# A fp32 encoder block on one core: weight loads through eight half-size buffers, with the pair loads in quarters

## The chip, the core and the metric

The kernel runs on one core of a Trainium2 chip. TensorE (PE) multiplies, with its weight loads shown as PEld; VectorE (DVE) and ScalarE (ACT) work on tiles in SBUF, which has 128 partitions; GpSimd (POOL) does a little; SyncE (SP) issues nearly all of the DMAs, one after another. The metric is the device time of one execution in microseconds, the median of several runs. Below, "us" is microseconds.

## What is computed

One layer of an encoder on 256 tokens of width 2048, in float32. The reference, cut to the order of the stages:

```
hn = rmsnorm(h, mix_norm_pre)
z, xbc, dt_raw, u = split(hn @ w_in)
mix = concat([ssd_mixer(z, xbc, dt_raw, ...), pool_mixer(u, ...)]) @ w_out
h = h + rmsnorm(mix, mix_norm_post)
hn = rmsnorm(h, ffn_norm_pre)
gate, val = split(hn @ w_ffn_up)                  # 2048 x 11264
ff = (gelu(dwconv(gate)) * val) @ w_ffn_down      # 5632 x 2048
h = h + rmsnorm(ff, ffn_norm_post)
gate = sigmoid(rmsnorm(h, ple_norm_pre) @ w_ple_gate)
h = h + rmsnorm(gate * (p @ w_ple), ple_norm_post)
```

Some 252 MB of weights and inputs are read from HBM in one execution.

## The kernel before

**Products.** Every weight tile is split in two parts: `split` (L147) casts it on ACT to a rounded high part (L152, names ending in `whi`) and subtracts that from it on DVE for the low part (L153, `wlo`). Activations are kept as such pairs too. A product of two fp32 matrices is then three products on PE: high x high, high x low, low x high, accumulated in PSUM. `mm` (L87) issues them all.

**Stages.** `w_in` first (names `dtu`, `xb`, `z`), then the mixers, then `wo` (the output projection), the FFN (`ug` and `uv`, the two halves of the up-projection, into `ga` and `va`), `dn` (the down-projection) and `gt` (the gate of the last step). In `dn` the output has two halves of 1024 columns, `dn0` and `dn1`; each runs over 22 units, and a unit is two row blocks of 128 rows by 1024 columns, 1 MB of weights. The number behind `dn0` or `dn1` in a name is the unit's first row block: `dn116` is unit 8 of the second half. PE writes its plain results to `dna` and four helper results to `dns`.

**Seven products.** Units 1, 3, 5, 6, 8, 10, 11, 13, 15, 16 (and 18 in the second half) of `dn`, and three units of `wo`, treat their 256 x 1024 weights as a 2 x 2 matrix of blocks b11, b12, b21, b22 of 128 x 512 and multiply in seven products instead of eight (`seven_products`, L224). This takes two weight combinations f and g (`weight_sums`, L214: one DVE operation for f, two for g) and sums of the activations (`hs`). The sums are made in the FFN stage, stored to DRAM, loaded back (`sums`, 256 KB) and split again. For the units with u % 5 = 3 (3, 8, 13, 18) f and g are made in `dn` from the raw load. For the others they are made in the FFN stage (`block_ahead`, from loads named `br`), stored, and loaded back as `bm` (1 MB); of the weights themselves `three_blocks` (L162) then loads only b12 and the row b21, b22.

The order of the seven is s4, a12 (both with the tile split from b21 and b22), a11 (with b11 or what stands for it), s1, s3 (f, the tile `c`), s2, a22 (g, the tile `d`), three matmuls of 128 x 512 each, on PE in this order.

**Buffers and queues.** A load goes to one of four raw buffers of 128 x 2048 (tag `raw`, 8 KB in each partition, L157 to L168). A buffer is free when the last operation on it has ended, and the load that waits for it blocks SP, with all loads behind it: SP's queue is in order. The split parts have five buffers each (tags `whi`, `wlo`), free when PE has read them. DMAs count on eight semaphores in turn, so each waits for the landing of the eighth before it. The scheduler of the tile framework lays each engine's instructions in one fixed order when the kernel is built, and the engines follow it in order.

**Front.** The first stage loads `x` in transposed form to three buffers (`xt0`, a raw buffer `xt1`, a page `xt2`; a page is another kind of buffer, 128 x 2048, 14 of them) and `w_in`'s columns for `dtu` to raw buffers and pages in turn.

Of the kernel before, what the change touches and what calls it, by code (L numbers as in the profile page):

```python
# [16 lines left out]
P = 128  # L17
L = 256
# [33 lines left out]
def build(nc, a, out):  # L52
# [5 lines left out]
    with tile.TileContext(nc) as tc, \  # L58
# [35 lines left out]
        make_identity(nc, ident)  # L94

        c_dt = DSSD + 1536
        r0 = wp.tile([P, 2048], F32, tag="raw", bufs=4, name="dtur0")
# [9 lines left out]
        for i in range(16):  # L107
            nc.tensor.transpose(warm[:, :P], ident, ident)

        xt = [ep.tile([P, V_SCW + L], F32, name="xt0")] + [wp.tile([P, 2048], F32, tag="raw", bufs=4, name="xt1"), page("xt2")]  # L110
        vt = cp.tile([P, V_N - V_SCW], F32, name="vt")
        small = ep.tile([P, 89 + 512], F32, name="small")

# [2 lines left out]
        def load(dst, src, ahead=False):  # L116

            with tc.issue_after(last["dma"]) if last and not ahead else nullcontext():
                return ins(nc.sync.dma_start(dst, src))

        def x_part(k):
            return xt[0][:, V_SCW:] if k == 0 else xt[1 + k // 9][:, (k - 1) % 8 * L:((k - 1) % 8 + 1) * L]

        def xload(k0, k1):
            c = ((k0 - 1) % 8) * L
            last["dma"] = load(xt[1 + k0 // 9][:, c:c + (k1 - k0) * L],
                               a["x_cols"][:, V_SCW + k0 * L:V_SCW + k1 * L])

        last["dma"] = load(xt[0], a["x_cols"][:, :V_SCW + L])
        dtb, alog, dsk = small[:, :32], small[:, 32:64], small[:, 64:80]  # L130
# [23 lines left out]
                c0 = c1  # L154
            return hi, lo

        def raw(name, src, a_, b_):  # L157
            r = wp.tile([P, 2048], F32, tag="raw", bufs=4, name=name)
            last["dma"] = load(r[:, :a_ * b_].rearrange("p (a b) -> p a b", a=a_), src, True)
            return r  # L160

        def three_blocks(name, w, k0, c0):  # L162

            r = wp.tile([P, 2048], F32, tag="raw", bufs=4, name=name)
# [48 lines left out]

        def weight_sums(name, r, dst=None):  # L214

            v = r.rearrange("p (b c) -> p b c", b=4)
            f, g = dst or (mid(f"{name}f"), mid(f"{name}g"))
            nc.vector.tensor_sub(f.rearrange("p (b c) -> p b c", b=2), v[:, 1:3],
                                 v[:, 0].unsqueeze(1).to_broadcast([P, 2, 512]))
            nc.vector.tensor_add(g[:, :512], v[:, 2], f[:, :512])  # L220
            nc.vector.tensor_sub(g[:, 512:], v[:, 3], g[:, :512])
            return f, g

        def seven_products(name, r, a_, acc, alt, start, stop, made=None):  # L224

            b2 = split(parts(f"{name}b"), r[:, 1024:], 0, 1024)
            b11 = split(parts(f"{name}a"), r[:, 512:], 0, 512)
            with tc.issue_after(last["dve"]) if name.startswith("wo") else nullcontext():
                f, g = made or weight_sums(name, r)
            t13, t24 = (split(parts(f"{name}{n}"), x, 0, 1024) for n, x in (("c", f), ("d", g)))  # L230
            for x, (wh, wl), c, o, own in (
                    ("s4", b2, 0, acc[0][0], False), ("a12", b2, 1, acc[0][1], False), ("a11", b11, 0, alt[0], True),
                    ("s1", t13, 0, alt[1], True), ("s3", t13, 1, alt[2], True), ("s2", t24, 0, alt[3], True),
                    ("a22", t24, 1, acc[1][1], False)):
# [19 lines left out]
            add(acc[1][0], acc[1][0], s165)  # L254
            add(acc[1][1], acc[1][1], s167)

        def pair_of_rows(w, k0, c0):
            return w[k0 * P:(k0 + 2) * P, c0:c0 + 1024].rearrange("(k p) c -> p k c", p=P), 2, 1024

        def split_two(name, w, k0, c0):  # L260

            r = raw(f"{name}r{k0}", *pair_of_rows(w, k0, c0))
            return [(k0 + j, *split(parts(f"{name}{k0}_{j}"), r[:, j * 1024:(j + 1) * 1024], 0, 1024)) for j in range(2)]

        def token_major(name, w, c0, ks, get, acc, tail=1, fast=(), alt=None, sums=None, hooks={}, made=None):


            group, nu, sums_of = [], len(ks) // 2, {}
            for u in range(nu):
                k0 = ks[2 * u]  # L270
                if u + 1 in fast:
                    sums_of[u + 1] = sums(ks[2 * u + 2])
                if u in fast:
                    sets = made(u, c0)
                    r = three_blocks(f"{name}r{k0}", w, k0, c0) if sets else raw(f"{name}r{k0}", *pair_of_rows(w, k0, c0))
# [24 lines left out]
        def feature_major(name, w, c0, get, acc):  # L300

            for u in range(4):
                r = raw(f"{name}r{u}", w[u * 512:(u + 1) * 512, c0:c0 + 512]
                        .rearrange("(k p) c -> p k c", p=P), 4, 512)
                tiles = []

                def step(j, kk, f):
# [5 lines left out]
                           k == 0 and q == 0 and f % 2 == 0, k == NK - 1 and q == 2)  # L313

                for j in range(2):
                    tiles.append(split(parts(f"{name}{u}_{j}"), r[:, j * 1024:(j + 1) * 1024], 0, 1024))
# [11 lines left out]
        def feature_pairs(name, w, c0, get, acc):  # L328
# [14 lines left out]
                        for kk in range(4) for f in range(2)]  # L343

            for u in range(2):
                r = raw(f"{name}r{u}", w[u * 1024:(u + 1) * 1024, c0:c0 + 256]
                        .rearrange("(k p) c -> p k c", p=P), 8, 256)
                tiles = []
                for j in range(2):
                    behind = held.pop((name, u, j), None)  # L350
                    with tc.issue_after(behind) if behind else nullcontext():
                        tiles.append(split(parts(f"{name}{u}_{j}"), r[:, j * 1024:(j + 1) * 1024], 0, 1024))
# [106 lines left out]


        for u in range(0, NK, 2):
            r = [wp.tile([P, 2048], F32, tag="raw", bufs=4, name=f"dtur{u}") if u else r0, page(f"dtur{u + 1}")]
            for j in range(2):
                k = u + j
                if k == 0:
# [6 lines left out]
                if k == 1:  # L472
                    xload(2, 4)
                elif k in (3, 5, 7):
                    xload(*{3: (4, 9), 5: (9, 13), 7: (13, 16)}[k])
# [349 lines left out]

        def wo_block(u):

            r = raw(f"wb{u}", *pair_of_rows(w_out, wo_ks[2 * u], 1024))
            v = page(f"wf{u}")
            wo_sets[u] = weight_sums(f"wb{u}", r, (v[:, :1024], v[:, 1024:]))  # L830

# [98 lines left out]

        def block_ahead(u, half):

            r = raw(f"br{u}_{half}", *pair_of_rows(w_down, 2 * u, half * 1024))
# [4 lines left out]
        def block_made(u, c0):  # L938
# [200 lines left out]
```

## Time and profile before

| | us |
|---|---|
| median of 3 runs | 1118.2 (1117.71 to 1118.35) |
| the profiled execution | 1121.51 |
| its span, first to last instruction | 1119.7 |
| PE busy | 1105.8 |
| DVE busy | 830.5 |
| ACT busy | 679.6 |

The profile is of one execution, the granted TensorE clock in it is 0.998 of full speed. Its parts are: busy time by engine, the span in slices, DMA queues, the chain of work that ended last (followed back from the end, at each step to what released it), the costliest groups of instructions, and the DMA issues with the time from issue to landing. Timelines give single instructions; a bracket at the end of a row tells how long the engine was idle before it and what released it. Times in rows are counted from the span's start.

### The profile page before, as it was taken

What the parts mean: (1) busy time and instruction counts of PE and PEld (TensorE: products, weight loads), DVE (VectorE), ACT (ScalarE), POOL (GpSimd) and SP (SyncE); (2) the same over time, 40 slices, a digit from 0 to 9 for tenths busy, and PEclk for the clock granted to TensorE, in tenths of its full rate; (3) what the DMA queues carried; (4) which work ended last, traced back from release to release, by engine and by line L of the source; (5) the groups of instructions that cost most, each with busy time, mean ns of one, the idle gap of its engine ahead of it and who ended that gap; (6) DMA issues with size and microseconds to landing.
All of it is one profiled execution on the core that took longest, in us unless ns stands there. A gap on an engine that the chain in (4) does not pass through costs nothing.

```text
span 1119.7 us, 15690 instructions
## 1 busy us (share of the span) xinstructions
PE 1105.8 (99%) x6032; PEld 962.3 (86%) x6032; DVE 830.5 (74%) x1040; ACT 679.6 (61%) x999; POOL 51.9 (5%) x80
## 2 busy tenths in 40 slices
PE   9999999999999999999999999999999999999996
PEld 9999988888788888888888888888888887877885
DVE  6668887879776876767767767666887787897574
ACT  6757884555865564655565656555666465657462
POOL 0300022100200000000000000000000000001001
PEclk9999999999999999999999999999999999999999
DMA  9954446666587977877897797676788778886742
GB/s 354 376 171 151 152 151 241 211 211 225 215 281 246 310 257 253 275 266 254 264 305 252 244 318 258 213 247 214 262 292 289 268 270 304 296 283 218 241 136 76
DMA packets 145739, 275.69 MB, mean 246 GB/s; under 512 B 5504, under 2 KB 98560, under 8 KB 142208
## 3 DMA queue, kind: packets, MB, share of 16 engines
q1 hardware_dynamic: 145376, 274.33, 72.8%
q8 instruction: 47, 0.77, 0.3%
q10 hardware_dynamic: 288, 0.36, 0.1%
q14 instruction: 28, 0.23, 0.1%
HBM read 251.86 MB, written 22.81 MB: 245 GB/s over the span
## 4 chain that ended last, share of the span: by engine, by line
PE 85%; DMA 7%; DVE 3%; ACT 2%; issue 2%; POOL 0%; SPq 0%; DVEq 0%; POOLq 0%; ACTq 0%
PE va L87 22%; PE ga L87 21%; PE dna L87 10%; PE gt L87 7%; PE woa L87 7%; PE xbc L87 6%; PE z L87 4%; PE dns L87 3%; DMA sums<-sums 2%; DMA dtur<-w_in 2%; DMA xb2r<-w_in 1%; DMA x<-x 1%; DMA dn1r<-w_ffn_down 1%; PE wos L87 1%; DVE dn_1wlo L153 1%
## 5 line engine op out<-in xcount | busy, mean ns | idle before, releaser
L87 PE MATMUL ga<-wox,ug_0whi 128*128 128x512 f32 x352 | 87.8, 391 | 0.0
L87 PE MATMUL va<-wox,uv_0whi 128*128 128x512 f32 x352 | 87.6, 391 | 0.0
L87 PE MATMUL ga<-wox,ug_1whi 128*128 128x512 f32 x352 | 87.2, 389 | 0.0
L87 PE MATMUL va<-wox,uv_1whi 128*128 128x512 f32 x352 | 86.9, 389 | 0.0
L87 PEld LDWEIGHTS va<-wox,uv_1whi 128*128 128x128 f32 x352 | 66.1, 188 | 13.7
L87 PEld LDWEIGHTS ga<-wox,ug_1whi 128*128 128x128 f32 x352 | 66.0, 188 | 13.7
L87 PEld LDWEIGHTS va<-wox,uv_0whi 128*128 128x128 f32 x352 | 64.6, 188 | 12.4
L87 PEld LDWEIGHTS ga<-wox,ug_0whi 128*128 128x128 f32 x352 | 64.6, 188 | 12.3
L87 PE MATMUL ga<-wox,ug_1wlo 128*128 128x256 f32 x352 | 49.7, 283 | 0.9 <-DVE ug_1wlo L153 0.9
L87 PE MATMUL ga<-wox,ug_0wlo 128*128 128x256 f32 x352 | 49.5, 283 | 0.0
L87 PE MATMUL va<-wox,uv_1wlo 128*128 128x256 f32 x352 | 49.4, 283 | 0.0
L87 PE MATMUL va<-wox,uv_0wlo 128*128 128x256 f32 x352 | 49.2, 283 | 0.0
L87 PEld LDWEIGHTS ga<-wox,ug_0wlo 128*128 128x128 f32 x352 | 46.8, 191 | 1.8
L87 PEld LDWEIGHTS va<-wox,uv_0wlo 128*128 128x128 f32 x352 | 46.7, 191 | 1.7
L87 PEld LDWEIGHTS ga<-wox,ug_1wlo 128*128 128x128 f32 x352 | 45.4, 192 | 1.3 <-DVE ug_1wlo L153 1.3
L87 PEld LDWEIGHTS va<-wox,uv_1wlo 128*128 128x128 f32 x352 | 45.4, 192 | 0.0
L87 PE MATMUL xbc<-hnh,xb_0whi 128*128 128x256 f32 x96 | 27.6, 288 | 0.3 <-ACT u L539 0.3
L864 POOL TENSOR_SCALAR dnm<-dnq,fmean 128x1 f32<-128x1 f32 x2 | 0.6, 282 | 587.5 <-ACT dnj L861 587.5
L87 PE MATMUL xbc<-hnh,xb_1whi 128*128 128x256 f32 x96 | 27.5, 287 | 0.0
L87 PE MATMUL xbc<-hnh,xb_0wlo 128*128 128x256 f32 x96 | 27.3, 284 | 0.0
L87 PE MATMUL xbc<-hnh,xb_1wlo 128*128 128x256 f32 x96 | 27.2, 283 | 0.0
L87 PE MATMUL xbc<-hnl,xb_1whi 128*128 128x256 f32 x96 | 27.2, 283 | 0.0
(1654 smaller groups left out, 3084.4 us busy)
## 6 DMA issues: line engine op xcount, KB each, us to landing
dn0r<-w_ffn_down SPq DMA_DIRECT2D x15, 1024.0 KB, 7.3
dn1r<-w_ffn_down SPq DMA_DIRECT2D x15, 1024.0 KB, 7.2
br<-w_ffn_down SPq DMA_DIRECT2D x14, 1024.0 KB, 5.5
bm<-block SPq DMA_DIRECT2D x14, 1024.0 KB, 5.5
zr<-w_in SPq DMA_DIRECT2D x8, 1024.0 KB, 5.2
wo0r<-w_out SPq DMA_DIRECT2D x8, 1024.0 KB, 6.0
gt0r<-w_ple_gate SPq DMA_DIRECT2D x8, 1024.0 KB, 5.9
gt1r<-w_ple_gate SPq DMA_DIRECT2D x8, 1024.0 KB, 5.5
```

The costliest lines, as they stand in the source:

```text
L87: last["pe"] = ins(nc.tensor.matmul(o, lhsT, rhs, start=start, stop=stop, skip_group_check=True))
L153: last["dve"] = ins(nc.vector.tensor_sub(lo[:, s], src[:, s], hi[:, s].bitcast(F32)))
L864: nc.gpsimd.tensor_scalar(m, q, 1.0 / D, mean[t], op0=ALU.mult, op1=ALU.add)
```

## The change

The four raw buffers of 128 x 2048 become eight of 128 x 1024, and each load of 1 MB becomes two or more, each into a buffer of its own with its own release.

- `split_two` (pairs of row blocks), `feature_major`, `feature_pairs` and the loads of `bm` take two loads of 512 KB in place of one of 1 MB.
- `four_blocks` takes the place of `three_blocks`, and of the whole load where f and g are made from it (`dn`, `block_ahead`, `wo_block`): four loads of 128 x 512 (256 KB), three where b11 isn't used. One buffer, r[1], holds b12 and b21; the other, r[0], holds b11 and b22. b12 and b21 are loaded first, then b22, then b11.
- `seven_products` splits r[1] whole first (tile `b`), then the b22 half of r[0] (tile `a`). s4 takes the second half of `b`, a12 the tile `a`, a11 the first half of `b`. f takes r[1] less b11, in one operation as before.
- In the front `xt1` and `xt2` become four half buffers, `dtur` lies in pages throughout, and one load of `x` is cut in two.

```
-            r = wp.tile([P, 2048], F32, tag="raw", bufs=4, name=name)
+            return wp.tile([P, 1024], F32, tag="raw", bufs=8, name=name)
...
-            load(r[:, 512:1024], w[k0 * P:(k0 + 1) * P, c0 + 512:c0 + 1024], True)
-            last["dma"] = load(r[:, 1024:], w[(k0 + 1) * P:(k0 + 2) * P, c0:c0 + 1024], True)
+            r = [buffer(f"{name}{i}") for i in range(2)]
+            for i, c, k in ((1, 0, 0), (1, 1, 1), (0, 1, 1), (0, 0, 0)):
+                if all_ or (i, c) != (0, 0):
+                    w0 = c0 + (c if i == 0 else 1 - c) * 512
+                    last["dma"] = load(r[i][:, c * 512:(c + 1) * 512], w[(k0 + k) * P:(k0 + k + 1) * P, w0:w0 + 512], True)
...
-            nc.vector.tensor_sub(f.rearrange("p (b c) -> p b c", b=2), v[:, 1:3],
-                                 v[:, 0].unsqueeze(1).to_broadcast([P, 2, 512]))
+            nc.vector.tensor_sub(f.rearrange("p (b c) -> p b c", b=2), r[1].rearrange("p (b c) -> p b c", b=2),
+                                 r[0][:, :512].unsqueeze(1).to_broadcast([P, 2, 512]))
...
-            b2 = split(parts(f"{name}b"), r[:, 1024:], 0, 1024)
-            b11 = split(parts(f"{name}a"), r[:, 512:], 0, 512)
+            mid_ = split(parts(f"{name}b"), r[1], 0, 1024)
+            end_ = split(parts(f"{name}a"), r[0], 512, 1024)
...
-                    ("s4", b2, 0, acc[0][0], False), ("a12", b2, 1, acc[0][1], False), ("a11", b11, 0, alt[0], True),
+                    ("s4", mid_, 1, acc[0][0], False), ("a12", end_, 1, acc[0][1], False), ("a11", mid_, 0, alt[0], True),
...
-            r = raw(f"{name}r{k0}", *pair_of_rows(w, k0, c0))
-            return [(k0 + j, *split(parts(f"{name}{k0}_{j}"), r[:, j * 1024:(j + 1) * 1024], 0, 1024)) for j in range(2)]
+            two = []
+            for k in (k0, k0 + 1):
+                r = raw(f"{name}r{k}", w[k * P:(k + 1) * P, c0:c0 + 1024])
+                two.append((k, *split(parts(f"{name}{k0}_{k - k0}"), r, 0, 1024)))
+            return two
...
-                r = raw(f"bm{x[0]}_{x[1]}", block[x].unsqueeze(1), 1, 2048)
-                return r[:, :1024], r[:, 1024:]
+                return [raw(f"bm{x[0]}_{x[1]}{i}", block[x][:, i * 1024:(i + 1) * 1024]) for i in range(2)]
```

SP's queue grows from 338 to 541 rows. The order on the other engines moves only in places. On DVE, in the second half of `dn` before the change, the splits of unit 6 (`dn112`: tiles b, a, c, d) stand ahead of f for unit 8 (`dn116f`), and the splits of unit 7 (`dn114_0`, `dn114_1`) behind it:

```order
L153 TENSOR_TENSOR dn112bwlo_8674<-dn1r12_8665,dn112bwhi_8673 128x1024
L153 TENSOR_TENSOR dn112awlo_8678<-dn1r12_8665,dn112awhi_8677 128x512
L153 TENSOR_TENSOR dn112cwlo_8682<-bm6_1_8671,dn112cwhi_8681 128x1024
L153 TENSOR_TENSOR dn112dwlo_8686<-bm6_1_8671,dn112dwhi_8685 128x1024
L218 TENSOR_TENSOR dn116f_8759<-dn1r16_8746 128x1024
L153 TENSOR_TENSOR dn114_0wlo_8715<-dn1r14_8712,dn114_0whi_8714 128x1024
L153 TENSOR_TENSOR dn114_1wlo_8719<-dn1r14_8712,dn114_1whi_8718 128x1024
```

The same place on DVE after the change:

```order
L162 TENSOR_TENSOR dn112bwlo_9079<-dn1r121_9067,dn112bwhi_9078 128x1024
L162 TENSOR_TENSOR dn112awlo_9083<-dn1r120_9066,dn112awhi_9082 128x512
L162 TENSOR_TENSOR dn112cwlo_9087<-bm6_10_9074,dn112cwhi_9086 128x1024
L230 TENSOR_TENSOR dn116f_9170<-dn1r161_9154,dn1r160_9153 128x1024
L162 TENSOR_TENSOR dn112dwlo_9091<-bm6_11_9076,dn112dwhi_9090 128x1024
L162 TENSOR_TENSOR dn114_0wlo_9120<-dn1r14_9117,dn114_0whi_9119 128x1024
L162 TENSOR_TENSOR dn114_1wlo_9126<-dn1r15_9123,dn114_1whi_9125 128x1024
```

f of unit 8 now stands one row earlier, ahead of the last split of unit 6. The same happens at f of units 3, 8 and 13 in the first half and 13 and 18 in the second. On ACT, in the second half of `dn` before the change, between the casts of g of unit 13 (`dn126d`) and of unit 15 (`dn130b`), `hs30` is the cast of unit 15's sums and `dn128` is unit 14:

```order
L152 CAST dn126dwhi_8983<-dn126g_8975 128x1024
L152 CAST dn128_0whi_9012<-dn1r28_9010 128x1024
L152 CAST hs30_9049<-sums30_9008 128x512
L152 CAST dn128_1whi_9016<-dn1r28_9010 128x1024
L152 CAST dn130bwhi_9054<-dn1r30_9046 128x1024
L152 CAST dn130awhi_9058<-dn1r30_9046 128x512
L152 CAST hs32_9094<-sums32_9044 128x512
```

The same place on ACT after the change:

```order
L161 CAST dn126dwhi_9410<-dn126g_9402 128x1024
L161 CAST hs30_9480<-sums30_9435 128x512
L161 CAST dn128_0whi_9439<-dn1r28_9437 128x1024
L161 CAST hs32_9529<-sums32_9473 128x512
L161 CAST dn128_1whi_9445<-dn1r29_9443 128x1024
L161 CAST dn130bwhi_9487<-dn1r301_9476 128x1024
L161 CAST dn130awhi_9491<-dn1r300_9475 128x512
```

The cast of `hs30` moves ahead of the first cast of unit 14, and that of `hs32` (unit 16) ahead of the second one; in the first half both move the same way. In the FFN the order on ACT and DVE stays, and PE's order stays but for the tiles `a` and `b` in the seven products.

More of the change, by code (lines that the diff above doesn't have):

```diff
@@ L96, in build, with buffer @@
         c_dt = DSSD + 1536
-        r0 = wp.tile([P, 2048], F32, tag="raw", bufs=4, name="dtur0")
+        def buffer(name):
+            return wp.tile([P, 1024], F32, tag="raw", bufs=8, name=name)
+        r0 = page("dtur0")
         for n in range(2):
@@ L108, in build @@
             nc.tensor.transpose(warm[:, :P], ident, ident)
-        xt = [ep.tile([P, V_SCW + L], F32, name="xt0")] + [wp.tile([P, 2048], F32, tag="raw", bufs=4, name="xt1"), page("xt2")]
+        xt = [ep.tile([P, V_SCW + L], F32, name="xt0")] + [buffer(f"xt{i}") for i in range(1, 5)]
         vt = cp.tile([P, V_N - V_SCW], F32, name="vt")
@@ L119, in load, with x_place @@
                 return ins(nc.sync.dma_start(dst, src))
+        def x_place(k):
+            return 1 + (k - 1) // 4, (k - 1) % 4 * L
         def x_part(k):
-            return xt[0][:, V_SCW:] if k == 0 else xt[1 + k // 9][:, (k - 1) % 8 * L:((k - 1) % 8 + 1) * L]
+            if k == 0:
+                return xt[0][:, V_SCW:]
+            i, c = x_place(k)
+            return xt[i][:, c:c + L]
         def xload(k0, k1):
-            c = ((k0 - 1) % 8) * L
-            last["dma"] = load(xt[1 + k0 // 9][:, c:c + (k1 - k0) * L],
-                               a["x_cols"][:, V_SCW + k0 * L:V_SCW + k1 * L])
+            i, c = x_place(k0)
+            last["dma"] = load(xt[i][:, c:c + (k1 - k0) * L], a["x_cols"][:, V_SCW + k0 * L:V_SCW + k1 * L])
         last["dma"] = load(xt[0], a["x_cols"][:, :V_SCW + L])
@@ L155, in split, with raw, four_blocks @@
             return hi, lo
-        def raw(name, src, a_, b_):
-            r = wp.tile([P, 2048], F32, tag="raw", bufs=4, name=name)
-            last["dma"] = load(r[:, :a_ * b_].rearrange("p (a b) -> p a b", a=a_), src, True)
-            return r
-        def three_blocks(name, w, k0, c0):
-            r = wp.tile([P, 2048], F32, tag="raw", bufs=4, name=name)
-            load(r[:, 512:1024], w[k0 * P:(k0 + 1) * P, c0 + 512:c0 + 1024], True)
-            last["dma"] = load(r[:, 1024:], w[(k0 + 1) * P:(k0 + 2) * P, c0:c0 + 1024], True)
+        def raw(name, src, a_=1):
+            r = buffer(name)
+            last["dma"] = load(r.rearrange("p (a b) -> p a b", a=a_) if a_ > 1 else r, src, True)
+            return r
+        def four_blocks(name, w, k0, c0, all_=True):
+            r = [buffer(f"{name}{i}") for i in range(2)]
[3 more added lines that the diff above has]
+                    last["dma"] = load(r[i][:, c * 512:(c + 1) * 512], w[(k0 + k) * P:(k0 + k + 1) * P, w0:w0 + 512], True)
             return r
@@ L255, in combine @@
             add(acc[1][1], acc[1][1], s167)
-        def pair_of_rows(w, k0, c0):
-            return w[k0 * P:(k0 + 2) * P, c0:c0 + 1024].rearrange("(k p) c -> p k c", p=P), 2, 1024
         def split_two(name, w, k0, c0):
-            r = raw(f"{name}r{k0}", *pair_of_rows(w, k0, c0))
-            return [(k0 + j, *split(parts(f"{name}{k0}_{j}"), r[:, j * 1024:(j + 1) * 1024], 0, 1024)) for j in range(2)]
+            two = []
[3 more added lines that the diff above has]
+            return two
         def token_major(name, w, c0, ks, get, acc, tail=1, fast=(), alt=None, sums=None, hooks={}, made=None):
@@ L274, in token_major @@
                     sets = made(u, c0)
-                    r = three_blocks(f"{name}r{k0}", w, k0, c0) if sets else raw(f"{name}r{k0}", *pair_of_rows(w, k0, c0))
+                    r = four_blocks(f"{name}r{k0}", w, k0, c0, not sets)
                 else:
@@ L302, in feature_major @@
             for u in range(4):
-                r = raw(f"{name}r{u}", w[u * 512:(u + 1) * 512, c0:c0 + 512]
-                        .rearrange("(k p) c -> p k c", p=P), 4, 512)
+                r = [raw(f"{name}r{u}{j}", w[u * 512 + j * 256:u * 512 + (j + 1) * 256, c0:c0 + 512]
+                         .rearrange("(k p) c -> p k c", p=P), 2) for j in range(2)]
                 tiles = []
@@ L315, in feature_major @@
                 for j in range(2):
-                    tiles.append(split(parts(f"{name}{u}_{j}"), r[:, j * 1024:(j + 1) * 1024], 0, 1024))
+                    tiles.append(split(parts(f"{name}{u}_{j}"), r[j], 0, 1024))
                     if u < 3:
@@ L345, in feature_pairs @@
             for u in range(2):
-                r = raw(f"{name}r{u}", w[u * 1024:(u + 1) * 1024, c0:c0 + 256]
-                        .rearrange("(k p) c -> p k c", p=P), 8, 256)
+                r = [raw(f"{name}r{u}{j}", w[u * 1024 + j * 512:u * 1024 + (j + 1) * 512, c0:c0 + 256]
+                         .rearrange("(k p) c -> p k c", p=P), 4) for j in range(2)]
                 tiles = []
@@ L351, in feature_pairs @@
                     with tc.issue_after(behind) if behind else nullcontext():
-                        tiles.append(split(parts(f"{name}{u}_{j}"), r[:, j * 1024:(j + 1) * 1024], 0, 1024))
+                        tiles.append(split(parts(f"{name}{u}_{j}"), r[j], 0, 1024))
                 for part in ((low, high) if u else (high, low)):
@@ L461, in build @@
         for u in range(0, NK, 2):
-            r = [wp.tile([P, 2048], F32, tag="raw", bufs=4, name=f"dtur{u}") if u else r0, page(f"dtur{u + 1}")]
+            r = [page(f"dtur{u}") if u else r0, page(f"dtur{u + 1}")]
             for j in range(2):
@@ L474, in build @@
                 elif k in (3, 5, 7):
-                    xload(*{3: (4, 9), 5: (9, 13), 7: (13, 16)}[k])
+                    for k0, k1 in {3: ((4, 5), (5, 9)), 5: ((9, 13),), 7: ((13, 16),)}[k]:
+                        xload(k0, k1)
                 elif k == 4:
@@ L826, in wo_block @@
         def wo_block(u):
-            r = raw(f"wb{u}", *pair_of_rows(w_out, wo_ks[2 * u], 1024))
+            r = four_blocks(f"wb{u}", w_out, wo_ks[2 * u], 1024)
             v = page(f"wf{u}")
@@ L931, in block_ahead @@
         def block_ahead(u, half):
-            r = raw(f"br{u}_{half}", *pair_of_rows(w_down, 2 * u, half * 1024))
+            r = four_blocks(f"br{u}_{half}", w_down, 2 * u, half * 1024)
             f, g = weight_sums(f"b{u}_{half}", r)
```

5 lines of the change are left out of this document (2 added, 3 removed).

## The prediction

> **What bounds the kernel now.** I read the page first: the span, the busy times and the shares of the chain of work that ended last.
>
> ```profile
> span 1119.7 us, 15690 instructions
> PE 1105.8 (99%) x6032; PEld 962.3 (86%) x6032; DVE 830.5 (74%) x1040; ACT 679.6 (61%) x999; POOL 51.9 (5%) x80
> PE 85%; DMA 7%; DVE 3%; ACT 2%; issue 2%; POOL 0%; SPq 0%; DVEq 0%; POOLq 0%; ACTq 0%
> ```
>
> PE is busy for 1105.8 of 1119.7 us. The change adds no product and takes none away, so it can give back at most the 14 us in which PE stands, and it loses wherever it makes PE wait. Next I asked for windows: the FFN's up-projections (304 to 784), the down-projection's first half (784 to 900) and second half (900 to 1012), and two short stretches of the second half. The columns are start and end, length, busy time (and instructions) of PE, PEld, DVE, ACT and POOL, the granted clock, the busy share of the DMA engines, GB/s.
>
> ```profile
> 304.00:784.00 480.00, 479.84 (x2766) 425.13 (x2767) 345.96 (x431) 282.36 (x420) 3.20 (x4) 1.00 0.80 262
> 784.00:900.00 116.00, 115.79 (x510) 95.28 (x510) 92.47 (x98) 70.22 (x84) 1.09 (x4) 1.00 0.82 281
> 900.00:1012.00 112.00, 110.22 (x480) 89.24 (x479) 91.94 (x98) 67.65 (x81) 0.93 (x3) 1.00 0.84 286
> 918.00:920.00 2.00, 2.00 (x10) 1.66 (x9) 2.00 (x3) 2.00 (x4) 0.00 (x0) 1.00 0.16 33
> 938.00:941.00 3.00, 3.00 (x15) 2.49 (x14) 1.80 (x3) 1.05 (x1) 0.00 (x0) 1.00 0.96 385
> ```
>
> The FFN and the first half leave PE no gap worth naming. Only the second half has one (110.22 of 112). There the DMA engines are nearly idle in one stretch (0.16 at 918) and full in another (0.96 at 938): loads come unevenly. The timeline of this half shows where PE stood. Its columns are start, length, engine, line, operation, tile written from the tiles read, and in brackets the wait ahead of it; "hs" are activation sums, "dn1r" a raw weight buffer, f a weight difference, "dn_0" the first tile of a unit without seven products.
>
> ```profile
> 931.40 0.39 PE L87 MATMUL dns<-dn112dwlo,hs 128*128 128x512 f32 x1
> 931.63 0.39 PE L87 MATMUL dns<-dn112dwhi,hs 128*128 128x512 f32 x1
> 932.76 0.39 PE L87 MATMUL dna<-dn_0whi,hidh 128*128 128x512 f32 x1
> 934.20 0.50 PE L87 MATMUL dna<-dn_0wlo,hidh 128*128 128x512 f32 x1 [1.05 <-DVE dn_0wlo L153]
> 944.08 0.61 PE L87 MATMUL dna<-dn_0whi,hidh 128*128 128x512 f32 x2
> 944.92 0.50 PE L87 MATMUL dna<-dn_0wlo,hidh 128*128 128x512 f32 x1 [0.22 <-DVE dn_0wlo L153]
> 956.88 0.39 PE L87 MATMUL dns<-dn122cwhi,hs 128*128 128x512 f32 x1
> 957.51 0.50 PE L87 MATMUL dns<-dn122cwlo,hs 128*128 128x512 f32 x1 [0.25 <-DVE dn122cwlo L153]
> ```
>
> Undisturbed products start 0.23 us apart (931.40, 931.63). By this spacing the three stalls cost 934.20 - 932.76 - 0.23 = 1.21, 944.92 - 944.08 - 2 x 0.23 = 0.38 and 957.51 - 956.88 - 0.23 = 0.40 us, and each first product after a stall takes 0.50 instead of 0.39: together 2.0 + 0.3 = 2.3 us. DVE and the load behind the largest, with the rows of DMA issues (engine, count, size, us from issue to landing) for a lone 256 KB load, a lone 1 MB load, and this one:
>
> ```profile
> 923.42 0.38 SPq L119 DMA_DIRECT2D dn1r<-w_ffn_down  x1
> 931.79 1.22 DVE L218 TENSOR_TENSOR dn116f<-dn1r 128x1024 f32<-128x1024 f32 x1 [2.86 <-DMA dn1r<-w_ffn_down]
> 932.93 1.22 DVE L153 TENSOR_TENSOR dn_0wlo<-dn1r,dn_0whi 128x1024 fp32r<-128x1024 f32 x1
> sums<-sums SPq DMA_DIRECT2D x1, 256.0 KB, 2.6
> bm<-block SPq DMA_DIRECT2D x1, 1024.0 KB, 4.9
> dn1r<-w_ffn_down SPq DMA_DIRECT2D x1, 1024.0 KB, 8.3
> ```
>
> The load for unit 8 goes out at 923.42, when the buffer's last reader (dn110dwlo) has ended, and lands 8.3 us later. DVE stands 2.86 us in front of f, and dn_0wlo, which PE needs, is queued behind f. The other two stalls are behind late sums, as the waits of this part of the run show for ACT (us in all, times, longest):
>
> ```profile
> ACT hs L152 <- DMA sums<-sums: 14.9, 9, 2.5
> ```
>
> **The change part by part.** The sum is made against the profiled execution (1121.5 us, span 1119.7), which lies 3.3 us above the median of 1118.2; I take differences from it and put them on the median.
>
> *Halves, earlier release.* A load of 1 MB now goes out as two of 512 KB or four of 256 KB, and the first of them when the first half of the buffer is free: behind dn110cwlo and not behind dn110dwlo, one DVE subtraction of 1.22 us earlier. What is left for the second half is half as much to move. From the rows, 768 KB more cost 4.9 - 2.6 = 2.3 us, so 512 KB cost 1.5 us. I call the advance of the last piece X and take X = 1.4 us; its bounds are 0 (four issues in a row, each behind the landing of the eighth load before it, eat it up) and 1.22 + 1.5 = 2.7. The gain if all three stalls go is 2.3 us.
>
> *Order.* With the shorter loads the order of DVE and ACT moves as well. On DVE the difference f of units 3, 8, 13 and 18 stands ahead of the last split of the unit before, which PE needs sooner. On ACT the sums of unit 15 (hs30) stand ahead of the casts of unit 14. So a late load now holds up something that it didn't hold up. The rows at these places, f or hs first and then PE's first use of what is now behind it:
>
> ```profile
> 815.95 1.23 DVE L218 TENSOR_TENSOR dn016f<-dn0r 128x1024 f32<-128x1024 f32 x1 [0.62 <-DMA dn0r<-w_ffn_down]
> 817.81 0.39 PE L87 MATMUL dns<-dn012dwlo,hs 128*128 128x512 f32 x1
> 841.76 1.23 DVE L218 TENSOR_TENSOR dn026f<-dn0r 128x1024 f32<-128x1024 f32 x1 [1.26 <-DMA dn0r<-w_ffn_down]
> 842.97 0.39 PE L87 MATMUL dns<-dn022dwlo,hs 128*128 128x512 f32 x1
> 985.23 1.22 DVE L218 TENSOR_TENSOR dn136f<-dn1r 128x1024 f32<-128x1024 f32 x1 [0.86 <-DMA dn1r<-w_ffn_down]
> 984.26 0.39 PE L87 MATMUL dns<-dn132dwlo,hs 128*128 128x512 f32 x1
> 853.56 0.62 ACT L152 CAST hs<-sums 128x512 fp32r<-128x512 f32 x1 [2.11 <-DMA sums<-sums]
> 854.09 1.05 ACT L152 CAST dn_1whi<-dn0r 128x1024 fp32r<-128x1024 f32 x1
> 854.76 0.62 PE L87 MATMUL dna<-dn_0wlo,hidh 128*128 128x512 f32 x2
> 970.59 0.62 ACT L152 CAST hs<-sums 128x512 fp32r<-128x512 f32 x1 [2.40 <-DMA sums<-sums]
> 970.79 0.61 PE L87 MATMUL dna<-dn_0wlo,hidh 128*128 128x512 f32 x2
> ```
>
> If nothing landed earlier (X = 0), f would start when it did, the split behind it 1.14 us later (931.79 to 932.93) and end after 1.22 more. The lateness against PE's use is 815.95 + 2.36 - 817.81 = 0.5 for unit 8 and 841.76 + 2.36 - 842.97 = 1.15 for unit 13 of the first half, 931.79 + 2.36 - 931.40 = 2.75 and 985.23 + 2.36 - 984.26 = 3.3 for units 8 and 18 of the second. (Unit 3 isn't late by its rows.) Behind hs30 come 0.53 us to the next cast (853.56 to 854.09), that cast (1.05) and its subtraction (1.22): 853.56 + 2.80 - 854.76 = 1.6 in the first half and 970.59 + 2.80 - 970.79 = 2.6 in the second. With X = 1.4 the remains are 0, 0, 1.35, 1.9, 0.2 and 1.2.
>
> They don't simply add: a stall of PE at one place makes every later tile of that half arrive earlier by as much against PE, as long as loads follow PE closely. So I count the largest of each half: 0.2 + 1.9 = 2.1 us. Against the 2.3 that go, the sum is -0.2 us.
>
> *Quarters of the pairs in another layout.* b11's split is now the second half of a buffer, and a12 needs it after three products instead of six. The nearest rows:
>
> ```profile
> 979.69 0.68 DVE L153 TENSOR_TENSOR dn132awlo<-dn1r,dn132awhi 128x512 fp32r<-128x512 f32 x1
> 980.64 0.39 PE L87 MATMUL dna<-dn132bwhi,hs 128*128 128x512 f32 x1
> ```
>
> The split ends at 980.37, and its new use is at 980.64 + 4 x 0.23 = 981.6: 1.2 us to spare. Elsewhere it has at least this much, except in unit 11 of the second half, where late sums push it to the edge. Cost 0, at most 0.4.
>
> *More DMAs.* SP issues 541 instead of 338, at 0.38 us each (923.42) 77 us more of a queue that mostly waits for buffers: 0, since the loads of 4 MB ahead cover it. Where four issues follow one another the last goes out 3 x 0.38 = 1.1 us after the first; that lies inside X's bounds. Packets of 2 KB instead of 4 KB may raise the engines' share. Shares of 0.80 to 0.84 leave room for 16% more work before they bound a stage.
>
> *FFN, wo, front.* The order of PE, DVE and ACT in the FFN doesn't move, and PE has lost 0.16 us there: 0, no gain possible. The front and the stage of wo have neither a moved step that waits for a load nor one of the three stalls: 0, with 0.5 either way.
>
> **The rivals.** *R1, slower: the earlier f and hs block their engines, and the waits add.* DVE stands in front of f with PE's next tile behind it, at four places, and ACT in front of hs30 at two. Added up, X = 1.4 gives 4.7 us, less 2.3: +2.4, 1120.6. X = 0.7 gives 0.45 + 2.05 + 2.6 + 0.9 + 1.9 = 7.9, less 2.3: +5.6, 1123.8. It decides for "slower" where the new waits exceed 4.5 us, that is when they add at X below 1.45. For it speaks that every f quoted waited for its load already from its later place; against it, that DMA engines had idle time ahead of these loads (0.16 at 918).
>
> *R2, faster: no new wait.* If release by halves lets loads run ahead by more than X = 2.7 in the second half, because each earlier split frees the next half earlier, all three stalls go: -2.3, 1115.9. Against it: hs30 and dn136f need an advance at the upper bound.
>
> *R3, slower: small loads are slow loads.* By the rows a load costs a fixed part, 2.6 - 0.77 = 1.8 us, and 1.5 us per 512 KB. If the fixed part held up the engines, two halves would take 2 x 3.3 = 6.7 us for 4.9, and the share of 0.80 in the FFN would become 1.1: about 0.1 x 480 = 48 us, 1166. Against it: from 938 to 941 loads of 256 and 512 KB, several under way at once, moved 385 GB/s at a share of 0.96, so fixed parts overlap. The Trainium skill, "DMA: Bandwidth & Descriptors", section "Measured (HBM→SBUF, 128 partitions, SWDGE, issued from GpSimd)", tells to batch DMAs to at least 1 MiB for at least 75% of peak; this change goes the other way throughout. By that rule alone R3 would be the forecast; this trace's 385 GB/s with small loads disagrees with it for loads that overlap, and I give it little.
>
> *R4: nothing moves.* If the stalls of the second half stay as they are and the new order costs nothing, 1118.2; this lies within the forecast's case.
>
> **How the numbers follow.** About 0.2% (2.2 us) is what a measurement of this kernel can tell from no change: below 1116.0 counts as faster, above 1120.4 as slower. Forecast (stalls exchanged for others of about the same size): -0.2, 1118.0, own range 1116.0 to 1120.4, chance 0.47. R1 0.27, taken at 1121.6 and tailing to 1123.8. R2 0.22, at 1115.9 and a little below, since the 2.3 us are nearly all that there is to gain. R3 0.04. So faster 0.22, same 0.47, slower 0.31. The range takes in R2's price with 0.3 us for the front (1115.6) and R1 up to where it counts one more wait of 1 us (1121.6); R3 and the rest of R1 stay outside, some 0.17, and 0.03 below.
>
> **What would show it.** In the changed profile: the loads for units 8, 13 and 18 land about 1.4 us earlier after their first issue than now; "dn116f" still waits for DMA, under 2.9 us; PE waits for dn112dwlo or dn132dwlo by 1 to 2 us, where dn_0wlo held it before; FFN windows with PE at 479.8 of 480 and a DMA share under 0.86. The forecast is wrong if the second half loses under 0.5 us on PE (R2), if waits of PE for the last splits, in both halves, sum to over 4.5 us (R1), or if the DMA share in the FFN rises towards 1 (R3).

## The result and the profile after

The changed kernel takes 1132.1 us (median of 6 runs, 1128.39 to 1138.14), the kernel before, run beside it, 1118.28 (6 runs, 1117.71 to 1124.54). The ratio is 1.0121, 95% interval 1.0105 to 1.0136: slower by 1.2%, and above the range that was forecast. The profiled execution took 1131.03 us, and its span is 9.5 us longer than that of before. The page of the changed kernel, the same three lines as of before:

```profile
span 1129.2 us, 16401 instructions
PE 1108.7 (98%) x6032; PEld 964.5 (85%) x6032; DVE 830.7 (74%) x1040; ACT 680.3 (60%) x999; POOL 53.0 (5%) x80
PE 82%; DMA 9%; DVE 3%; ACT 3%; issue 2%; SPq 1%; POOL 0%; DVEq 0%; POOLq 0%; ACTq 0%
```

DMA's share of the chain grew from 7 to 9% and PE's fell. The windows of the FFN, the two halves of the down-projection, and two short stretches behind stalls (columns as before):

```profile
304.00:784.00 480.00, 479.86 (x2766) 425.17 (x2767) 345.66 (x431) 282.13 (x420) 3.17 (x4) 1.00 0.85 262
784.00:900.00 116.00, 111.34 (x480) 90.78 (x479) 87.07 (x92) 65.64 (x74) 0.00 (x0) 0.99 0.80 265
900.00:1012.00 112.00, 108.21 (x468) 88.36 (x468) 89.74 (x96) 68.47 (x84) 1.09 (x4) 0.98 0.87 286
848.40:852.40 4.00, 3.74 (x9) 2.96 (x10) 4.00 (x5) 1.04 (x1) 0.00 (x0) 0.57 0.58 167
940.90:944.40 3.50, 3.21 (x8) 2.53 (x9) 3.50 (x4) 0.67 (x1) 0.00 (x0) 0.52 0.87 290
```

The FFN loses nothing, although its DMA share rose from 0.80 to 0.85. PE now stands in both halves of the down-projection, where before only the second had gaps. In the two last rows PE hardly stands at all, but its granted clock is 0.57 and 0.52. PE's timeline of the changed kernel shows the places:

```profile
817.96 0.39 PE L87 MATMUL dns<-dn012dwhi,hs 128*128 128x512 f32 x1
818.39 0.50 PE L87 MATMUL dns<-dn012dwlo,hs 128*128 128x512 f32 x1
843.97 0.39 PE L87 MATMUL dns<-dn022dwhi,hs 128*128 128x512 f32 x1
848.66 0.63 PE L87 MATMUL dns<-dn022dwlo,hs 128*128 128x512 f32 x1 [4.30 <-DVE dn022dwlo L162]
849.08 0.63 PE L87 MATMUL dns<-dn022dwhi,hs 128*128 128x512 f32 x1
938.68 0.39 PE L87 MATMUL dns<-dn112dwhi,hs 128*128 128x512 f32 x1
941.19 0.79 PE L87 MATMUL dns<-dn112dwlo,hs 128*128 128x512 f32 x1 [2.12 <-DVE dn112dwlo L162]
992.95 0.39 PE L87 MATMUL dns<-dn132dwhi,hs 128*128 128x512 f32 x1
994.55 0.50 PE L87 MATMUL dns<-dn132dwlo,hs 128*128 128x512 f32 x1 [1.21 <-DVE dn132dwlo L162]
```

Each of the four stalls is a wait for the last split (`d`) of the unit ahead of one whose f is made here. Less the usual spacing of 0.23 us they cost 0.20, 4.46, 2.28 and 1.37 us. After the second and third, products start 0.42 us apart (848.66, 849.08) instead of 0.23. By the granted clock this lost about 0.43 x 4.0 + 0.48 x 3.5 = 3.4 us more. Together 11.7 us; the 2.3 us of stalls of before are gone; 9.4 is left of the 9.5 us by which the span grew.

DVE's timeline shows what the split waited for: f, which now stands ahead of it and waits for its load.

```profile
815.98 1.23 DVE L230 TENSOR_TENSOR dn016f<-dn0r,dn0r 128x1024 f32<-128x1024 f32 x1 [1.63 <-DMA dn0r<-w_ffn_down]
846.24 1.23 DVE L230 TENSOR_TENSOR dn026f<-dn0r,dn0r 128x1024 f32<-128x1024 f32 x1 [5.88 <-DMA dn0r<-w_ffn_down]
847.38 1.22 DVE L162 TENSOR_TENSOR dn022dwlo<-bm,dn022dwhi 128x1024 fp32r<-128x1024 f32 x1
938.77 1.23 DVE L230 TENSOR_TENSOR dn116f<-dn1r,dn1r 128x1024 f32<-128x1024 f32 x1 [3.70 <-DMA dn1r<-w_ffn_down]
992.14 1.23 DVE L230 TENSOR_TENSOR dn136f<-dn1r,dn1r 128x1024 f32<-128x1024 f32 x1 [2.79 <-DMA dn1r<-w_ffn_down]
```

The second row is the worst: DVE does nothing for 5.88 us, although the cast of `dn022d` is ready, and that split starts only at 847.38, behind f.

### The profile page after: what moved, and what is told of

It is laid out like the page before. It is cut to its first block, busy times and chain, and to the rows that moved or that the text cites. A ratio compares the mean times of both kernels' runs of the same rounds, so it can differ in the third digit from the quotient of the medians.

```text
span 1129.2 us, 16401 instructions
## 1 busy us (share of the span) xinstructions
PE 1108.7 (98%) x6032; PEld 964.5 (85%) x6032; DVE 830.7 (74%) x1040; ACT 680.3 (60%) x999; POOL 53.0 (5%) x80
## 4 chain that ended last, share of the span: by engine, by line
PE 82%; DMA 9%; DVE 3%; ACT 3%; issue 2%; SPq 1%; POOL 0%; DVEq 0%; POOLq 0%; ACTq 0%
PE ga L87 21%; PE va L87 21%; PE dna L87 8%; PE gt L87 7%; PE woa L87 7%; PE xbc L87 6%; PE z L87 4%; PE dns L87 2%; DMA dn1r<-w_ffn_down 2%; DMA dn0r<-w_ffn_down 2%; DMA sums<-sums 2%; DMA dtur<-w_in 1%; DMA x<-x 1%; PE wos L87 1%; DVE dn_0wlo L162 1%
```

## The experiments

Theory A was that the order did it: f at the head of DVE's queue waits for a load, and the split that PE needs stands behind it. Theory B was that halves and quarters land later, whatever the order. Later questions were whether quarters or halves cost the rest (C and D), and what the moved casts of the sums cost. All ratios are to the kernel before, timed on the same chip.

| kernel | us, median | ratio (95% interval) |
|---|---|---|
| changed | 1132.1 | 1.0121 (1.0105 to 1.0136) |
| changed, f put back | 1124.3 | 1.0045 (1.0029 to 1.0061) |
| same, quarters joined to two loads | 1127.35 | 1.0073 (1.0047 to 1.0098) |
| f put back, b11 loaded third | 1122.3 | 1.0028 (1.0014 to 1.0041) |
| f put back, whole rows for quarters | 1120.65 | 1.0015 (1.0006 to 1.0024) |
| changed, f latest | 1121.24 | 1.0020 (1.0009 to 1.0030) |
| f latest, sums' casts put back | 1119.22 | 1.0003 (0.9995 to 1.0012) |
| same, whole rows for quarters | 1119.6 | 1.0013 (1.0004 to 1.0022) |
| before, f early | 1126.47 | 1.0068 (1.0048 to 1.0088) |
| before, f latest | 1117.43 | 0.9994 (0.9984 to 1.0003) |
| the same again, five rounds | 1117.46 | 0.9988 (0.9979 to 0.9998) |

**f put back, the loads as changed.** The edit, in `seven_products`:

```
-            with tc.issue_after(last["dve"]) if name.startswith("wo") else nullcontext():
+            behind = last["dve"] if name.startswith("wo") else last.get("d")
+            with tc.issue_after(behind) if behind else nullcontext():
                 f, g = made or weight_sums(name, r)
             t13, t24 = (split(parts(f"{name}{n}"), x, 0, 1024) for n, x in (("c", f), ("d", g)))
+            last["d"] = last["dve"]
```

> The changed kernel with one edit: on DVE, f of units 3, 8, 13 and 18 stays behind the last split of the fast unit before, as in the kernel before. All loads stay as the change made them. Theory A (the order: a late load at the head of DVE's queue holds up a split that PE needs): the three stalls at the last splits and the slower clock behind them go, and the time returns to 1117 to 1120. Theory B (the loads: halves and quarters land later, whatever the order): the splits of the loaded tiles are late all the same, 1127 or more.

It gave 1124.3, between the two: f's place is worth 0.76 of the 1.21%, and 0.45% is left that theory A doesn't explain. The profiled execution, the fastest of nine, shows little of it (one longer wait of PE in the down-projection, 0.9 us), so the same kernel was profiled again:

> The kernel with f put back once more, for a second profile: its first one (1120.67) was the fastest of nine, whose median was 1124.3. If the rest over before comes from loads that land late in some executions, this profile shows waits of PE for splits in the down-projection that the first lacks; if it comes from another stage, the losses of PE lie there.

This execution took 1124.30, the median. PE's waits in the down-projection of this second profile (us in all, times, longest); one more, for sums, is 0.5 us:

```profile
PE dna L87 <- DVE dn_0wlo L162: 4.7, 3, 2.5
```

DVE in the same execution, f of unit 13 in the first half:

```profile
844.78 1.22 DVE L230 TENSOR_TENSOR dn026f<-dn0r,dn0r 128x1024 f32<-128x1024 f32 x1 [4.29 <-DMA dn0r<-w_ffn_down]
```

In the kernel before, this f starts at 841.76: its load is late also with f behind the last split, and PE meets it one tile later, at `dn_0wlo`, which stands behind f. For the two first of the three waits this is so in the kernel before too. The third (0.87 us, ending at 989.15) is at unit 17 of the second half: there, and at unit 12 of that half, `dn_0wlo` stood ahead of f before, and this run doesn't bring that back.

**The order alone, in the kernel before.** Loads and buffers are those of before. The raw loads of the next two units and f are emitted between the splits `c` and `d` of the unit two ahead, and `d` issued behind f. In the second half this moves f of units 3 and 13 ahead of a `d` too, which the change doesn't do:

```
+            t13 = split(parts(f"{name}c"), f, 0, 1024)
+            behind = between() if between else None
+            with tc.issue_after(behind) if behind else nullcontext():
+                t24 = split(parts(f"{name}d"), g, 0, 1024)
```

> The kernel before, whole loads of 1 MB in four buffers, with the order alone moved: f of units 3, 8, 13 and 18 ahead of the last split of the fast unit before. Theory A: slower by about the lateness that the rows of before give, 6 to 12 us, 1124 to 1130, with PE waiting for the last splits of units 6, 11 and 16. Theory B: within 3 us of before, 1121 or less, since whole loads aren't late.

0.68% slower, 7.6 us by the ratio, as theory A said, and about what putting f back won in the changed kernel. This kernel also moves some casts of sums, and in the second half it moves PE's order: a few products of units 7 and 8 stand ahead of the product that needs the last split. So only the first half shows the wait for the split by itself. In the second half PE waits first for a cast of unit 8's own load, and the split of `dn112d` ends at 938.40, just behind that wait. The two longest of PE's waits in its profile (two more, for the same cast of units 13 and 18, are 0.7 and 0.8 us):

```profile
PE dns L87 <- DVE dn022dwlo L153: 2.8, 1, 2.8
PE dns L87 <- ACT dn116awhi L152: 1.7, 1, 1.7
```

**Quarters joined in pairs, f put back.** One load of two blocks by a stride, for each half buffer:

```
+                    src = bass.AP(b.tensor, b.offset, [list(b.ap[0]), [P * w.shape[1] + 512 - 2 * c, 2], list(b.ap[1])])
+                    last["dma"] = load(r[i].rearrange("p (b c) -> p b c", b=2), src, True)
```

> As the run with f put back, and the four quarter loads of a pair of row blocks put together to two of 512 KB in the same layout (rows of 2 KB in both). Theory A: the same as with f put back, within 1.5 us. Theory B: faster than with f put back by 2 us or more, since fewer loads are under way.

Not faster: 1.0073 against 1.0045, intervals overlapping. So fewer loads gave no gain; whether joining them costs, these four runs don't show.

**b11 third, f put back.** The order of the four loads alone:

```
-            for i, c, k in ((1, 0, 0), (1, 1, 1), (0, 1, 1), (0, 0, 0)):
+            for i, c, k in ((1, 0, 0), (1, 1, 1), (0, 0, 0), (0, 1, 1)):
```

> The kernel with f put back to its place of before, and the quarter b11, which f needs, loaded third instead of last. If f waits for the last of four quarters, issued up to 2.2 us after the first, f starts about 0.6 us earlier in each of four places per half: 1121.5 to 1123.5 against 1124.3 with b11 last. If the wait is for the engines as a whole (all four land together), no change within 0.1%.

1122.3, the expected direction and size, though the intervals (1.0014 to 1.0041, 1.0029 to 1.0061) overlap, so this stays likely and isn't shown. In its profile f of unit 13 starts at 841.26; in the first profile with b11 last, also of the fastest execution, it starts at 842.22.

```profile
841.26 1.23 DVE L230 TENSOR_TENSOR dn026f<-dn0r,dn0r 128x1024 f32<-128x1024 f32 x1 [0.87 <-DMA dn0r<-w_ffn_down]
```

**Whole rows in halves, f put back.** Two loads of 512 KB, the layout of before, f in two operations:

```
+            for i in range(2):
+                c = 0 if i or all_ else 512
+                last["dma"] = load(r[i][:, c:], w[(k0 + i) * P:(k0 + i + 1) * P, c0 + c:c0 + 1024], True)
...
+            nc.vector.tensor_sub(f[:, :512], r[0][:, 512:], r[0][:, :512])
+            nc.vector.tensor_sub(f[:, 512:], r[1][:, :512], r[0][:, :512])
```

> Half buffers, but no quarter loads: each row block of a pair is one load of 512 KB with rows of 4 KB, the layout of before (f then takes two DVE operations of 512 columns instead of one of 1024), with f behind the last split as before. Putting f back left 0.45% over the kernel before. Theory C (the quarters, their count and their rows of 2 KB, cost the rest): within 0.2% of before, 1117 to 1121. Theory D (the halves themselves cost it, since more loads are under way and finish later): 1122 or more.

1.0015, in the bounds of theory C. But here f's first operation needs only the first row block, and the second stands later in the queue; so this run takes away the quarters and part of f's wait at once. The next runs part the two.

**f latest.** f goes behind the splits of the unit between and its own two, in the changed kernel and in the kernel before:

```
-            with tc.issue_after(last["dve"]) if name.startswith("wo") else nullcontext():
+            behind = last["dve"] if name.startswith("wo") else last.get("two")
+            with tc.issue_after(behind) if behind else nullcontext():
...
                     two = ready.pop(name) if u == 0 and name in ready else split_two(name, w, k0, c0)
+                    last["two"] = last["dve"]
```

> The changed kernel with f later than ever: behind the splits of the unit between and so behind the unit's own two splits. Theory A: no split of an earlier unit stands behind a late load, so PE waits for none of these; 1116 to 1119, unless f becomes late for its own products, which would show as waits for tile c of units 8, 13 and 18. Theory B: 1127 or more.

1121.24, so 0.20% over before and not at or below it. Its first profile, again the fastest execution, has no stall in the down-projection. A second profile:

> The kernel with f latest once more, for a second profile: the first (1117.7) was the fastest of ten with a median of 1121.2. Where a slower execution loses its 3 to 4 us: in waits of the down-projection (loads) or elsewhere (front or the stage of the output projection).

It took 1120.25. ACT in the second profile, at unit 14 of the second half:

```profile
967.56 0.62 ACT L161 CAST hs<-sums 128x512 fp32r<-128x512 f32 x1 [3.77 <-DMA sums<-sums]
968.09 1.04 ACT L161 CAST dn_0whi<-dn1r 128x1024 fp32r<-128x1024 f32 x1
```

And PE there:

```profile
969.18 0.73 PE L87 MATMUL dna<-dn_0whi,hidh 128*128 128x512 f32 x2 [0.93 <-ACT dn_0whi L161]
```

This is the other move of order: the cast of unit 15's sums stands ahead of unit 14's first cast, and ACT stands 3.77 us in front of it for a load of 256 KB. PE loses 0.93 us here and 0.53 at the next tile. Undoing this move too (`one` and `a` are the casts that the two stood behind):

```
+                with tc.issue_after(last[{30: "one", 32: "a"}[k]]) if k in (30, 32) else nullcontext():
+                    split((o[:, 512:], o), s, 0, 512)
```

> The kernel with f latest (halves and quarters kept) with the second move of order undone too: the casts of the sums of units 15 and 16 stand behind the casts that they stood behind before the change. With f latest alone, the time was 0.2% over before, and its second profile lost 1.8 us at unit 14's first tile, behind the sums of unit 15. If the order of these casts is the rest: within 0.1% of before, 1117 to 1119. If the halves and quarters have a cost of their own: 1120 or more still.

1.0003 (0.9995 to 1.0012): with f late and the sums' casts put back, the kernel with halves and quarters can't be told from the one before. But f stands later here than before the change, and what that is worth by itself the last two runs tell. With whole rows instead of quarters:

> The same, f latest and the sums' casts put back, with half buffers but whole rows of 512 KB in place of quarters. If quarters cost something beyond the wait of f, this is faster than the run with quarters by 0.1% or more; if f's wait was their whole cost, both are the same within 0.1%. The best version with halves: 1116 to 1118.

1.0013, not faster than with quarters. So the runs show no cost of the quarters beyond f's wait for the last of them. The kernel before with f latest:

> The kernel before with one edit: f of units 3, 8, 13 and 18 behind the splits of the unit between and its own two. Theory A: the stall of 1.2 us in front of dn_0wlo goes and nothing new comes, 1 to 2 us faster than before, 1116 to 1118. Rival: f and so tile c are too late for their own products, slower by 1 us or more.

> The kernel before with f behind the unit's own splits, once more and in five rounds: the first time gave 0.9994 (0.9984 to 1.0003) of the kernel before, though its profile has none of the stalls at the splits that the profile of before has (2.3 us, 0.2%). If such stalls stand in most executions of before, 0.998 to 0.999; if the profile of before (1121.5, over its median of 1118.2) was one of the slower executions, no difference within 0.1%.

The first time couldn't be told from no change; the second gave 0.9988 (0.9979 to 0.9998), about 1.3 us faster. The windows of its second profile, both halves of the down-projection:

```profile
784.00:900.00 116.00, 116.00 (x513) 96.06 (x512) 93.80 (x98) 71.06 (x86) 1.10 (x4) 1.00 0.82 282
900.00:1012.00 112.00, 112.00 (x496) 92.48 (x495) 96.94 (x102) 71.60 (x86) 3.40 (x6) 1.00 0.84 289
```

PE stands in neither. This version, with its four large buffers, has the lowest ratio of all.

The account, from differences of ratios and so good to about 0.15% each: f's early place 0.76%, f's wait for the quarters, still ahead of `dn_0wlo`, 0.25% (0.45 to 0.20), the sums' casts 0.17% (0.20 to 0.03), the rest 0.03%. Two limits go with it. With f put back, f of units 13 and 18 in the second half still stood ahead of a `dn_0wlo` that it stood behind before, so the 0.25% holds some order too. (For unit 13 there, this is the whole move of the change: its f stays behind the last split.) And the rest of 0.03% sets a kernel with f latest against one without. Against the kernel before with f latest (0.9994 and 0.9988) halves and quarters are 0.09 and 0.15% slower, the second just clear of noise: that they cost nothing isn't shown.

## Why the prediction was wrong

**The mechanism and its places were named, as the rival R1.** f of the units 8, 13 and 18 holds the last split, which PE waits for; the hs of unit 15 holds unit 14's cast. The first was shown by undoing it, and by moving f in the kernel before; for the second, of which the profile after has no wait of PE, stand ACT's row above and the run that undid it, whose interval still touches that of the run without it (1.0009 to 1.0012). But the forecast gave R1 0.27, and its dearest case, 1123.8, lies under the fastest run, 1128.39.

**The step that failed is X, the advance of the last piece, taken as 1.4 us with bounds of 0 and 2.7.** The formula around it held. With f's start in the changed kernel, 2.36 us for f and the split, and PE's due time (0.23 us behind the product ahead of the stall), the lateness is 815.98 + 2.36 - 818.19 = 0.15, 846.24 + 2.36 - 844.20 = 4.40, 938.77 + 2.36 - 938.91 = 2.2 and 992.14 + 2.36 - 993.18 = 1.3 us; the stalls were 0.20, 4.46, 2.28 and 1.37. The prediction had 0.5, 1.15, 2.75 and 3.3 for X = 0. So X was 0.35, -3.25, 0.5 and 2.0: never the same, and once far below the lower bound. The prediction gave no reason that excludes an advance below 0.

**Why X could be negative.** The estimate let loads go out earlier because buffers come free earlier. It forgot that a buffer is freed by the same queue in which f stands, and took the smaller last piece to land sooner. DVE ahead of unit 13, in the changed kernel:

```profile
832.29 1.22 DVE L162 TENSOR_TENSOR dn020bwlo<-dn0r,dn020bwhi 128x1024 fp32r<-128x1024 f32 x1
```

and in the kernel before:

```profile
829.65 1.22 DVE L153 TENSOR_TENSOR dn020bwlo<-dn0r,dn020bwhi 128x1024 fp32r<-128x1024 f32 x1
```

DVE is 2.6 us later there, where PE is only 844.20 - 842.97 = 1.2 us later. 1.2 of the 2.6 us stand already at the last split of unit 8 (824.72 before, 825.88 after); then DVE stands 1.35 us for a cast of sums that had no such wait before. On SP in the changed kernel, the first and the last quarter for unit 13:

```profile
835.88 0.33 SPq L123 DMA_DIRECT2D dn0r<-w_ffn_down  x1
837.95 0.55 SPq L123 DMA_DIRECT2D dn0r<-w_ffn_down  x1
```

and the whole load for unit 13 in the kernel before:

```profile
835.81 0.38 SPq L119 DMA_DIRECT2D dn0r<-w_ffn_down  x1
```

The first quarter does wait for one subtraction less (`dn020cwlo` instead of `dn020dwlo`), but with DVE late it goes out no earlier than the whole load did. The last one goes out 2.1 us later, and f needs all four. It also takes longer from issue to landing than the load of 1 MB:

```profile
dn0r<-w_ffn_down SPq DMA_DIRECT2D x1, 256.0 KB, 8.2
dn0r<-w_ffn_down SPq DMA_DIRECT2D x1, 1024.0 KB, 5.9
```

2.1 + 8.2 - 5.9 = 4.4 us, nearly all of the 846.24 - 841.76 = 4.5 by which f starts later. The DMA engines from 830 to 838, changed kernel:

```profile
830.00:838.00 8.00, 7.79 (x35) 6.13 (x34) 7.89 (x9) 6.41 (x8) 0.00 (x0) 1.00 0.77 228
```

and before:

```profile
830.00:838.00 8.00, 8.00 (x37) 6.60 (x37) 6.35 (x8) 5.25 (x6) 0.00 (x0) 1.00 0.90 294
```

The engines moved less just before the late load, at a share of 0.77 against 0.90.

f's early place isn't needed for a late load, though. In the second profile with f put back, the last quarter goes out at 836.85 and lands 7.8 us later, f starts 3.0 us later than in the kernel before (844.78), and the engines' share in this stretch is 0.79. In the first profile of the same kernel f starts only 0.5 us later (842.22). So the lateness differs from one execution to the next. How much of it the late release, the quarters and their slower landing each make wasn't measured apart: that part of the cause stays open. The run with b11 third bears on the quarters' share without showing it.

**Counting only the largest stall of each half failed too.** The stalls of units 8 and 18 in the second half, 2.28 and 1.37, both stand in the same execution. By the rows there was a lead, but too small a one. Between these two units f stays about 6.9 us behind its start in the kernel before (938.77 - 931.79 and 992.14 - 985.23), while PE's due time goes from 7.5 to 8.9 us behind (938.91 - 931.40 and 993.18 - 984.26). That is a gain of 1.4 us against the 3.3 by which unit 18 was late for X = 0.

**What the sum lacked:** the slow clock behind long stalls, about 3.4 us, which it put at nothing without a reason.

**What held:** the FFN without loss (479.86 of 480, share 0.85, under the 0.86 that was named), so R3 was wrong; the issues of SP, since joining quarters brought nothing; and the earlier need for tile `a`, for which no wait of PE appears in the profile after. The 2.3 us that could be won were the profile's; in the runs, f latest won 0.7 (not clear of noise) and 1.3 (0.06 and 0.12%).

**What held with a wrong reading.** From 938 to 941 a load of 1 MB was under way too (`bm`, issued at 935.31, 6.0 us to landing), so these 385 GB/s don't show small loads alone. The FFN after does: 262 GB/s, as before, with weight loads of 256 and 512 KB. The traces count 342 and 607 DMA issues on SP, so 265 more and not 203; at 0.38 us each that is 101 us, still without a cost that the runs show. And a12's first product is three spacings behind 980.64, not four, so 0.95 us were to spare and not 1.2.

## What to carry to other kernels

On an in-order engine, an operation that waits for a load sets the time of everything behind it, the releases that let later loads start among them. So when a scheduler moves such an operation up, price the move at the lateness seen in the trace, added up over the places, and allow for loads that get later. Put such an operation as late as its own reader allows, before buffers are cut finer: here that was worth more than the finer buffers.

## What the runs showed of the hardware

After a stall of 2.28 us, and after one of 4.46, PE ran at half its clock for 3.4 us: products 0.42 us apart, and a granted clock of 0.50 in these two stretches of the changed kernel:

```profile
848.88:852.29 3.41, 3.41 (x9) 2.65 (x9) 3.41 (x4) 1.04 (x1) 0.00 (x0) 0.50 0.61 175
941.05:944.45 3.40, 3.26 (x8) 2.58 (x9) 3.40 (x4) 0.72 (x1) 0.00 (x0) 0.50 0.87 286
```

Two more profiles have such a stretch: the order alone from 847.17 to 850.56, with PE idle for 2.79 us up to 845.98, and joined quarters from 993.00 to 996.39, with 3.18 us idle up to 993.26. The second profile with f put back has a wait of 2.49 us, up to 847.19, and no slow clock around it:

```profile
843.00:851.00 8.00, 5.51 (x25) 4.24 (x24) 6.22 (x7) 1.67 (x2) 0.00 (x0) 1.00 0.77 278
```

So the length of the stall alone doesn't decide. The Trainium skill, "TensorE: Matmul & The Clock Gate", section "Part 1: The HAM clock gate (the "warmup" mystery)", tells of a free-running window of about 3.4 us and of a drop to half after at least one idle window. The 3.4 us at half clock agree with the window; but a stall of 2.28 us, shorter than one window, was enough here.

An estimate from these rows: the two slow stretches of the changed kernel start 92.2 us apart, 27 times 3.413 us, which fits windows of that length laid end to end. In the windows just ahead of the four slow stretches PE was idle for 3.2, 2.0, 2.2 and 3.2 us. In the execution that kept its clock, windows counted back from its drop at the end (1118.50) have a border at 845.43, which cuts the wait of 2.49 us into 0.7 and 1.8. So about 2 us of idle time within one window was enough, and 1.8 was not; what lies between, and whether idle time is what counts, no run here tests.
